# The last 256 feed-forward columns by seven products of quarters, and the products added up in a tree of bank copies

## The chip, the cores and the metric

The kernel runs on one core of a Trainium2 chip. The metric is the device time of one execution in microseconds (us). Before the change the median of three runs is 909.1 us (909.03 to 910.12).

Five engines take part, each with an instruction queue of its own that it works off in order: TensorE (PE, matmuls into PSUM banks), VectorE (DVE), ScalarE (ACT), GpSimd (POOL) and SyncE (SP). Here SP issues nearly all loads of weights; POOL issues those loads that add onto what a buffer holds.

## The reference

Two layers, each with a feed-forward stage, a mixing stage (attention, two kinds of heads) and a second feed-forward stage; 256 tokens of width 1024, feed-forward width 2816, all fp32. The change touches the four feed-forward stages alone:

```python
D_MODEL = 1024; SEQ = 256; DEPTH = 2; D_FF = 2816

def swiglu(h, w_gate, w_up, w_down):
    return (jax.nn.silu(h @ w_gate) * (h @ w_up)) @ w_down

for l in range(DEPTH):
    x = x + 0.5 * swiglu(rms_norm(x, ffn1_norm[l]), ffn1_w_gate[l], ffn1_w_up[l], ffn1_w_down[l])
    ...   # mixing stage: x = x + concat(oA, oB) @ W_out
    x = x + 0.5 * swiglu(rms_norm(x, ffn2_norm[l]), ffn2_w_gate[l], ffn2_w_up[l], ffn2_w_down[l])
return rms_norm(x, final_norm)
```

## The kernel before, in words

**Precision.** Every fp32 operand is held as two fp32r parts, high and low. A product of 128 rows is three matmuls: high by high, low by high, high by low. For a weight buffer (`raw`) ACT casts the high part and DVE subtracts it to get the low part; these are the tiles `w`, and one such half of a buffer (128x1024) is called a split. The 256 tokens stand in two blocks of 128.

**A feed-forward stage.** The 2816 columns go in five groups of 512 and a last 256. For each group the kernel makes gate and up products (over 1024 rows, in two halves of 512 rows), the hidden values silu(gate) x up, transposes them on PE, and adds the down product into four banks that stay open for the stage. The down product of a group comes one to two groups later: `below(old, g - 2, 1, ...)` is the right half (dn1) of the group two back, `below(by_token(new), g - 1, 0, ...)` the left half (dn0) of the group one back, for which the transposes (`turn_one`) are made and evicted in the same group: ACT copies the high part out of the bank, DVE takes the low part.

**Seven products of quarters.** Groups 1 to 4 (2 to 4 in the first stage) replace the eight products gate/up x two row halves x two token blocks by seven (`by_sevens`, Strassen's scheme in Winograd's form). The four quarters of the weights are a (gate, top rows), b (up, top), c (up, bottom), d (gate, bottom). The seven products take the weights a, d, c and the sums b+c, a+b, a+b+c, a+b+c+d; the x side has sums of its own (`q` and `v`), made in `make_sums`. Sums of weights are made in two ways: a *gather* is a load by POOL that adds b onto a's buffer once a has been split, or c onto b's once b has been loaded; the sums with c and with d are made by a DVE addition over the whole buffer (`raw<-raw,raw`, 128x2048).

**Order.** Each engine's instructions are recorded in program order; nothing reorders them afterwards. `specs` lists the weight buffers of the whole kernel as steps. `ahead(n)` splits buffers up to half-buffer n ahead of what PE has used, and with them issues the loads and the sums' preparation; how far ahead it runs at each place is read from the table `LEAD` by stage (`first`, `mid`, `last` for groups, `open`, `close`), through `go()`. So these numbers set where on DVE and ACT a split stands among the evictions. There are six `raw` buffers.

**The last 256 columns** go by plain products: one buffer holds 256 gate and 256 up columns side by side, so that one 512-wide matmul makes both. That is 24 matmuls for the top rows, the transposes of group 4 (`turn(h, 2)`, 8 of them), and 24 for the bottom rows:

```python
gu = pair()
tokens(gu, norm.xs, weights(), 0)
hT = turn(h, 2)
tokens(gu, norm.xs, weights(), 4)
h = hidden(gate([b[:, 0:256] for b in gu]), [b[:, 256:512] for b in gu])
```

Names in the profile: every engine instruction is recorded in one helper, line 62 before and line 77 after, so rows are told apart by tiles. `ps` and `xy` are PSUM banks, `w` weight parts, `raw` loaded weights, `s` tiles of x or of hidden values and their parts, `q` and `v` sums of x, `tmp` scratch for silu and sums, `hr` half of the norm factor.

## Time and profile before

| | before |
|---|---|
| median of three runs | 909.1 us |
| profiled execution: span | 907.5 us |
| its own time | 909.1 us: the span and some 1.6 us around it |
| PE busy | 899.1 us, 99% |
| DVE busy | 785.9 us, 87% |
| ACT busy | 609.8 us, 67% |
| POOL busy | 63.2 us, 7% |
| one group of 512 columns on PE, second stage | 30.8 us |
| last 256 columns on PE, second stage | 11.8 us |
| matmul and transpose instructions on PE | 4468 |

The page gives for each engine its busy time, the share of the span and the number of instructions. The chain that ended last is followed back from the last instruction, and an engine's share of it tells how much of the span hung on it. In a row of groups, "out<-in" names tiles, the numbers before the bar are shape and count, those behind it the busy us, the mean ns of one, and the idle time just before with the one who ended it. In a timeline, brackets at a row's end hold the idle time before it and who ended that. The granted PE clock is at full speed in all forty slices of the page.

The feed-forward stages lie at 8.7 to 188 us, 285.6 to 458.4, 458.4 to 634 and 731.4 to 896.5; the mixing stages are in between.

### The profile page before, as it was taken

The page shows a single profiled execution, that of the slowest core. Times are in us where ns is not written, and L with a number is a line of the kernel's source. Part 1 is how long each engine was busy: PE and PEld are TensorE (multiplying, and loading weights), DVE is VectorE, ACT ScalarE, POOL GpSimd, SP SyncE. Part 2 cuts the span into 40 slices and gives each one's busy share as a digit, 9 for nine tenths or more (in the row PEclk, how much of TensorE's full clock was granted, in tenths as well). Part 3 has the DMA queues.
Part 4 walks back from the last instruction along what each step waited for, and adds up shares of the span by engine and source line. Part 5 has one row for each costly group of instructions (what it writes and reads, how often), then busy time and mean ns, then how long its engine had stood idle before and what let it go on. Part 6 is the DMA issues. An engine that isn't in the chain of part 4 may idle for free.

```text
span 907.5 us, 12030 instructions
## 1 busy us (share of the span) xinstructions
PE 899.1 (99%) x4468; PEld 751.0 (83%) x4468; DVE 785.9 (87%) x1069; ACT 609.8 (67%) x970; POOL 63.2 (7%) x79
## 2 busy tenths in 40 slices
PE   9999999999999999999999999999999999999997
PEld 7888888888888888888888888888888888888886
DVE  5968999879987899999778999988888978999894
ACT  6946677666776776677575776667667785776660
POOL 0401000000001001000000001000000000101011
PEclk9999999999999999999999999999999999999999
DMA  9998897954148798897976898899611786898731
GB/s 328 355 287 213 236 309 247 268 143 179 47 150 241 174 265 247 247 300 256 279 204 171 250 278 258 252 303 248 182 57 48 263 223 166 234 312 255 219 114 47
DMA packets 114331, 200.83 MB, mean 221 GB/s; under 512 B 3678, under 2 KB 31648, under 8 KB 114272
## 3 DMA queue, kind: packets, MB, share of 16 engines
q1 hardware_dynamic: 97616, 167.66, 54.4%
q0 software_dynamic: 16096, 31.75, 20.1%
q8 instruction: 35, 0.57, 0.2%
q10 hardware_dynamic: 560, 0.66, 0.2%
q14 instruction: 24, 0.20, 0.1%
HBM read 199.00 MB, written 1.05 MB: 220 GB/s over the span
## 4 chain that ended last, share of the span: by engine, by line
PE 98%; DMA 1%; issue 0%; SPq 0%; DVE 0%; POOLq 0%; POOL 0%
PE ps L62 73%; PE xy L62 25%; DMA xk<-in_x_dram 1%; SPq L172 0%; DVE s L62 0%; DVE xk L62 0%; POOLq L1285 0%; POOL rf L62 0%; SPq L469 0%; SPq L465 0%; DVE tot L62 0%; DVE tmp L62 0%
## 5 line engine op out<-in xcount | busy, mean ns | idle before, releaser
L62 DVE TENSOR_TENSOR w<-raw,w 128x1024 fp32r<-128x1024 f32 (+1 forms) x458 | 476.4, 1097 | 34.6 <-ACT w L62 33.2
L62 PE MATMUL ps<-w,s 128*128 128x512 f32 (+1 forms) x2046 | 473.6, 389 | 0.0
L62 PEld LDWEIGHTS ps<-w,s 128*128 128x128 f32 x2046 | 379.9, 188 | 78.7 <-issue 0.8
L62 ACT CAST w<-raw 128x1024 fp32r<-128x1024 f32 (+1 forms) x457 | 403.9, 954 | 54.0 <-DVE raw L62 38.7
L62 PE MATMUL xy<-w,s 128*128 128x512 f32 x528 | 125.8, 392 | 0.0
L62 PEld LDWEIGHTS xy<-w,s 128*128 128x128 f32 x528 | 98.2, 188 | 20.4
L62 PE MATMUL xy<-w,q 128*128 128x512 f32 x360 | 88.1, 393 | 0.0
L62 PEld LDWEIGHTS xy<-w,q 128*128 128x128 f32 x360 | 66.5, 188 | 13.3
L62 PE MATMUL ps<-s,w 128*128 128x512 f32 (+1 forms) x384 | 69.8, 338 | 0.0
L62 DVE TENSOR_TENSOR raw<-raw,raw 128x2048 f32<-128x2048 f32 x30 | 68.6, 2288 | 0.5
L62 POOL DMA_DIRECT2D raw<-in_ffn_w_up_dram x30 | 38.9, 1313 | 430.1 <-DVE w L62 264.9
L62 PEld LDWEIGHTS ps<-s,w 128*128 128x128 f32 x384 | 58.6, 188 | 8.5
L62 ACT ACTIVATE s<-ps,gcol 128x256 fp32r<-128x256 f32 (+1 forms) x80 | 31.4, 479 | 34.0 <-PE ps L62 34.0
L62 ACT CAST s<-ps 128x512 fp32r<-128x512 f32 x36 | 20.4, 592 | 43.2 <-PE ps L62 43.0
L62 PE MATMUL ps<-w,q 128*128 128x512 f32 x180 | 43.2, 389 | 0.0
L62 PE MATMUL ps<-w,v 128*128 128x512 f32 x180 | 43.2, 389 | 0.0
L62 DVE TENSOR_TENSOR s<-ps,s 128x512 fp32r<-128x512 f32 x36 | 24.1, 686 | 19.5 <-ACT s L62 19.3
L62 PEld LDWEIGHTS ps<-w,v 128*128 128x128 f32 x180 | 33.8, 188 | 7.0
L62 PEld LDWEIGHTS ps<-w,q 128*128 128x128 f32 x180 | 33.8, 188 | 7.0
L62 ACT ACTIVATE s<-s,negm 128x256 f32<-128x256 f32 x64 | 31.8, 498 | 5.3 <-DVE negm L62 5.3
L62 ACT COPY ps<-ps 128x512 f32<-128x512 f32 x15 | 8.6, 570 | 34.4 <-PE ps L62 34.4
L62 DVE SCALAR_TENSOR_TENSOR s<-ps,gcol,s 128x256 fp32r<-128x256 f32 x48 | 20.3, 477 | 13.0 <-ACT s L62 12.9
(131 smaller groups left out, 584.3 us busy)
## 6 DMA issues: line engine op xcount, KB each, us to landing
raw<-in_ffn_w_down_dram SPq DMA_DIRECT2D x44, 1024.0 KB, 7.0
raw<-in_ffn_w_gate_dram SPq DMA_DIRECT2D x39, 1024.0 KB, 7.7
raw<-in_ffn_w_up_dram SPq DMA_DIRECT2D x39, 1024.0 KB, 7.1
raw<-in_ffn_w_up_dram POOLq DMA_DIRECT2D x30, 1024.0 KB, 10.0
raw<-in_w_in_dram SPq DMA_DIRECT2D x14, 1024.0 KB, 6.7
raw<-in_ffn_w_gate_dram SPq DMA_DIRECT2D x8, 512.0 KB, 7.9
raw<-in_ffn_w_up_dram SPq DMA_DIRECT2D x8, 512.0 KB, 8.9
raw<-in_w_in_dram SPq DMA_DIRECT2D x8, 512.0 KB, 6.0
```

What stands on the lines that cost most here:

```text
L62: ins = issue(*a, **k)
```

## The change

It has four parts.

1. **The last 256 columns go by seven products too.** Two buffers are loaded: r (the gate's 256 columns, top and bottom rows side by side) and q (up's). DVE makes all sums itself, on 128x4x256 halves. Seven products of 12 matmuls of 256 columns replace 48 of 512.
2. **Products accumulate in a tree of bank copies.** Four banks, A, B, Q and Y, are used over and over. The product with a is made in A, copied to Q and added to there by d: that is the first block's gate. a+b+c goes on into A, which is copied to Y, b+c into A again, which is copied to Q; c goes onto Y, a+b into B. The last product, a+b+c+d, goes onto Q and is the second block's gate at once, so one DVE subtraction per group falls away. The sign moves into `nhr`, minus half the norm factor.
3. **The weights of a group come in another order** (`ORDER`): a, dn1, d, dn0, a+b, a+b+c, b+c, c, a+b+c+d, before a, dn1, b+c, dn0, d, a+b, c, a+b+c, a+b+c+d. PE takes a+b+c ahead of a+b (`taker`). The gather c onto b is issued right behind the gather b onto a; before, some 10 us lay between them. c's own buffer is loaded beside the step of a+b (`also`).
4. **The table `LEAD` is new**, with entries for each stage and for the last 256 columns (`edge`); `make_sums` makes the sums of x in another order; the transposes of x go as matmuls with the transpose flag, one start and stop per bank.

The diff, cut; in `by_seven` the calls of `go()` and `flat()` are left out, and the words behind # are added here:

```diff
+ORDER = (("a", "d", "dn0", "ab", "abc", "bc", "c", "abcd"),
+         ("a", "dn1", "d", "dn0", "ab", "abc", "bc", "c", "abcd"))
...
-            mid=(2, 8, 12, 12, 15, 15, 20, 20, 20, 22, 23),
+            more1=(6, 9, 9, 11, 11, 15, 19, 19, 19, 24, 24),
+            edge1=(2, 7, 7, 9, 9, 11, 12, 12),
...
-        steps[0].prep = lambda: issue(gather(b, a), 1)
-        return [Step(4, 512, load(a), key=a, free=[])] + steps + [
-                Step(4, 512, None, src=a, free=[]),
-                Step(4, 512, load(c), key=c, free=[]),
-                Step(4, 512, None, prep=plus(c, a), src=a, free=[c], early=1),
-                Step(4, 512, None, prep=plus(d, a), src=a, free=[a, d])]
+        parts = dict(a=Step(4, 512, load(a), key=a, free=[]),
+                     d=Step(4, 512, load(d), key=d, free=[]),
+                     ab=Step(4, 512, None, src=a, free=[], also=(c, load(c))),
+                     abc=Step(4, 512, None, prep=plus(c, a), src=a, free=[]),
+                     bc=Step(4, 512, load(b), key=b, added=True),
+                     c=Step(4, 512, None, src=c, added=False),
+                     abcd=Step(4, 512, None, prep=plus(d, a), src=a, free=[a, d], early=2))
...
+        steps[steps.index(parts["a"]) + 1].prep = lambda: issue(gather(b, a), 1)
+        steps[steps.index(parts["d"]) + 1].prep = begin          # gather(c, b)
...
+    def small(wg, wu):
+        r, q = object(), object()
+        left, right = slice(0, 256), slice(256, 512)
+        def load(w):
+            return lambda t: [(t[:, :, h * 256:h * 256 + 256], rows(w, FF - 256, 256, 4 * h, 4)) for h in range(2)]
+        def plus(x, b, to, a):
+            dve.tensor_tensor(raws[to][:, :, a], raws[to][:, :, a], raws[x][:, :, b], op=ALU.add)
+        def pairs():
+            plus(q, left, r, left)
+            plus(q, right, q, left)
+        return [Step(4, 512, load(wg), key=r, src=r, free=[], pick=((r, left), (r, right))),
+                Step(4, 512, None, prep=pairs, src=r, free=[], also=(q, load(wu)), added=False, pick=((r, left), (q, left))),
+                Step(4, 512, None, prep=lambda: plus(q, right, r, left), src=r, free=[q], added=False, pick=((r, left), (q, right))),
+                Step(4, 512, None, prep=lambda: plus(r, right, r, left), src=r, free=[r], added=False, pick=((r, left), None))]
...
-                p1 = prod(norm.quarter(0, 0), take())
-                act.activation(xy[0], p1, AF.Copy, scale=-1.0)
...
-                g1 = flat()
-                dve.tensor_tensor(g1, p4, u1, op=ALU.subtract)
-                silu(g1, g1, 1)
+        def by_seven(banks, take, go, then):
+            A, B, Q, Y = banks
+            prod(norm.quarter(0, 0), take("a"), A, True)
+            act.copy(Q, A)
+            then("a")                                            # dn1, transposes
+            prod(norm.quarter(0, 1), take("d"), Q)
+            g0 = silu(flat(), Q, 0)
+            then("d")                                            # dn0
+            prod(norm.summed(1), take("abc"), A)
+            act.copy(Y, A)
+            prod(norm.summed(0), take("ab"), B, True)
+            act.copy(e, B)
+            prod(norm.summed(2), take("bc"), A)
+            act.copy(Q, A)
+            dve.tensor_tensor(u1, A, e, op=ALU.add)
+            prod(norm.summed(3), take("c"), Y)
+            dve.tensor_tensor(u0, Y, e, op=ALU.add)
+            up(h, u0, g0, 0, norm.nhr)
+            prod(norm.quarter(1, 1), take("abcd"), Q)
+            g1 = silu(flat(), Q, 1)
+            up(h, u1, g1, 1, norm.nhr)
...
-        gu = pair()
-        tokens(gu, norm.xs, weights(), 0)
-        hT = turn(h, 2)
-        tokens(gu, norm.xs, weights(), 4)
-        h = hidden(gate([b[:, 0:256] for b in gu]), [b[:, 256:512] for b in gu])
+            A, B, Q, Y = [b[:, 0:256] for b in banks]            # the same seven, 256 wide
+            wa = take()
+            prod(norm.quarter(0, 0), wa, 0, A, True)
+            act.copy(Q, A)
+            for t in range(2):
+                new.append(turn_one(h, t, banks[1 + 2 * t]))
+            prod(norm.quarter(0, 1), wa, 1, Q)
...
+            prod(norm.quarter(1, 1), take(), 0, Q)
```

**Three places in the instruction order.** First PE at the last 256 columns of the second feed-forward stage. Before, the end of the top rows' matmuls, the transposes of group 4 and the start of the bottom rows (`xy_4021` and `xy_4022` are the two token blocks' banks):

```order
L62 MATMUL xy_4022<-w_3965,s_525_2779 128x512 x2
L62 MATMUL xy_4022<-w_3966,s_525_2779 128x512
L62 MATMUL ps_4064<-ident,s_774_3949 128x128 x4
L62 MATMUL ps_4072<-ident,s_774_3949 128x128 x4
L62 MATMUL xy_4021<-w_3973,s_537_2834 128x512 x2
L62 MATMUL xy_4021<-w_3974,s_537_2834 128x512
L62 MATMUL xy_4022<-w_3973,s_537_2834 128x512 x2
L62 MATMUL xy_4022<-w_3974,s_537_2834 128x512
```

After, the end of the first product (a, in `ps_3039`), the transposes into the banks `xy_3041` and `xy_3042`, the product with d (into `ps_3040`) and the start of the third:

```order
L77 MATMUL ps_3039<-w_3932,s_523_2826 128x256 x2
L77 MATMUL ps_3039<-w_3933,s_523_2826 128x256
L77 MATMUL xy_3041<-ident,s_768_4000 128x128 x4
L77 MATMUL xy_3042<-ident,s_768_4000 128x128 x4
L77 MATMUL ps_3040<-w_3952,s_537_2885 128x256 x2
...
L77 MATMUL ps_3040<-w_3952,s_539_2895 128x256 x2
L77 MATMUL ps_3040<-w_3953,s_539_2895 128x256
L77 MATMUL ps_3039<-w_4016,q_2957 128x256 x2
L77 MATMUL ps_3039<-w_4017,q_2957 128x256
```

The matmuls are 256 wide, and the same four banks serve as in the groups.

Second DVE in group 4 of the same stage. Before, with `raw_3471` and `raw_3608` the down weights, `raw_3523` b with c on it, `raw_3659` d and `raw_3463` a, which at its end holds a+b:

```order
L62 TENSOR_TENSOR w_3710<-raw_3471,w_3709 128x1024
L62 TENSOR_TENSOR w_3714<-raw_3523,w_3713 128x1024
L62 SCALAR_TENSOR_TENSOR s_720_3693<-tmp_3689,hr_2897,tmp_3707 128x512
L62 TENSOR_TENSOR w_3722<-raw_3523,w_3721 128x1024
L62 TENSOR_TENSOR w_3767<-raw_3608,w_3766 128x1024
L62 TENSOR_TENSOR w_3771<-raw_3608,w_3770 128x1024
L62 TENSOR_TENSOR s_737_3782<-ps_3777,s_737_3782 128x512
L62 TENSOR_TENSOR s_738_3789<-xy_2999,s_738_3789 128x512
L62 TENSOR_TENSOR w_3793<-raw_3659,w_3792 128x1024
L62 TENSOR_TENSOR w_3797<-raw_3659,w_3796 128x1024
L62 TENSOR_TENSOR w_3801<-raw_3463,w_3800 128x1024
L62 TENSOR_TENSOR w_3805<-raw_3463,w_3804 128x1024
```

After, with `raw_3649` the weights of dn0, `raw_3501` a (from its third row here a+b, then with `raw_3681`, c, added), `raw_3683` b with c on it:

```order
L77 TENSOR_TENSOR w_3748<-raw_3649,w_3747 128x1024
L77 SCALAR_TENSOR_TENSOR s_709_3728<-tmp_3712,nhr_2950,tmp_3765 128x512
L77 TENSOR_TENSOR w_3806<-raw_3649,w_3805 128x1024
L77 TENSOR_TENSOR w_3810<-raw_3501,w_3809 128x1024
L77 TENSOR_TENSOR w_3814<-raw_3501,w_3813 128x1024
L77 TENSOR_TENSOR raw_3501<-raw_3501,raw_3681 128x2048
L77 TENSOR_TENSOR s_729_3825<-xy_3041,s_729_3825 128x512
L77 TENSOR_TENSOR s_730_3832<-xy_3042,s_730_3832 128x512
L77 TENSOR_TENSOR w_3836<-raw_3501,w_3835 128x1024
L77 TENSOR_TENSOR w_3840<-raw_3501,w_3839 128x1024
L77 TENSOR_TENSOR w_3844<-raw_3683,w_3843 128x1024
```

The two evictions of the transposes (`s<-ps,s` and `s<-xy,s` before, `s<-xy,s` after) stood ahead of the splits of a+b; now they stand behind these and behind the addition of c.

Third DVE at the last 256 columns. Before, splits of plain buffers and the evictions of the transposes:

```order
L62 TENSOR_TENSOR w_4002<-raw_3901,w_4001 128x1024
L62 TENSOR_TENSOR w_4024<-raw_3901,w_4023 128x1024
L62 TENSOR_TENSOR w_4028<-raw_3903,w_4027 128x1024
L62 TENSOR_TENSOR w_4032<-raw_3903,w_4031 128x1024
L62 TENSOR_TENSOR s_802_4069<-ps_4064,s_802_4069 128x2x256
L62 TENSOR_TENSOR s_804_4077<-ps_4072,s_804_4077 128x2x256
L62 SCALAR_TENSOR_TENSOR s_807_4108<-xy_4021,hr_2897,tmp_4104 128x256
L62 SCALAR_TENSOR_TENSOR s_807_4108<-xy_4022,hr_2897,tmp_4106 128x256
```

After, with `raw_3818` r and `raw_3856` q:

```order
L77 TENSOR_TENSOR w_3933<-raw_3818,w_3932 128x1024
L77 TENSOR_TENSOR w_3953<-raw_3818,w_3952 128x1024
L77 TENSOR_TENSOR raw_3818<-raw_3818,raw_3856 128x4x256
L77 TENSOR_TENSOR raw_3856<-raw_3856 128x4x256
L77 TENSOR_TENSOR tmp_3973<-ps_3039,tmp_3950 128x512
L77 TENSOR_TENSOR w_3976<-raw_3818,w_3975 128x1024
L77 TENSOR_TENSOR w_3980<-raw_3856,w_3979 128x1024
L77 TENSOR_TENSOR raw_3818<-raw_3818,raw_3856 128x4x256
L77 TENSOR_TENSOR tmp_3998<-xy_3042,tmp_3950 128x512
L77 SCALAR_TENSOR_TENSOR s_768_4000<-tmp_3998,nhr_2950,tmp_3871 128x512
L77 TENSOR_TENSOR w_4017<-raw_3818,w_4016 128x1024
```

Sums and splits of r and q alternate, with the two bank sums (`tmp`) and the hidden values (`s`) of group 4 among them.

More of the change, by code (lines that the diff above doesn't have):

```diff
@@ L129, in plain, with seven @@
         return Step(kn, n, lambda t: [(t, src)], **how)
-    def seven(wg, wu, c0, below, down):
+    def seven(wg, wu, c0, order):
         a, b, c, d = [object() for _ in range(4)]
@@ L296, in ffn_specs @@
                 if g in sevens:
[L297 removed]
+                    specs.extend(seven(wg[l], wu[l], g * 512, [dict(dn1=down(g - 2, 1) if g > 1 else None, dn0=downs[0]).get(o, o)
+                                                                  for o in ORDER[g > 1]]))
                     if g == max(sevens):
@@ L812, in turn @@
+        def turn(hs, n, into=None):
             out_ = []
-            for i in (range(n) if isinstance(n, int) else n):
-                sl = halves(bank())
+            for i in range(n):
+                sl = halves(into[i] if into else bank())
                 for c in range(2):
@@ L870, in ffn @@
             g = gate(gs)
-            next(sums)
         else:
```

308 lines of the change are left out of this document (185 added, 123 removed).

## Prediction

> **What bounds the kernel.** I read the page first (busy shares, then the shares of the chain that ended last), then what TensorE (PE) waited for.
>
> ```profile
> span 907.5 us, 12030 instructions
> PE 899.1 (99%) x4468; PEld 751.0 (83%) x4468; DVE 785.9 (87%) x1069; ACT 609.8 (67%) x970; POOL 63.2 (7%) x79
> PE 98%; DMA 1%; issue 0%; SPq 0%; DVE 0%; POOLq 0%; POOL 0%
> PE ps L62 <- DVE wake L62: 1.0, 1, 1.0
> PE ps L62 <- DMA xk<-in_x_dram: 0.7, 1, 0.7
> ```
>
> PE is on the chain for 98% of the span, and all its waits are two, 1.7 us together, in the opening. So nothing can be won by ending a wait: the change gains only what it takes off PE's stream, and loses whatever new wait it makes. VectorE (DVE) at 87% is the engine to watch, since the change gives it more to do and writes its work in another order.
>
> The chain in order of time shows PE's stream of the second feed-forward stage (start, length, what):
>
> ```profile
> 309.20 10.88 PE ps L62 x48
> ...
> 340.01 10.88 PE ps L62 x48
> ...
> 401.65 10.88 PE ps L62 x48
> ...
> 426.13 5.45 PE xy L62 x24
> 431.58 0.87 PE ps L62 x8
> 432.45 5.47 PE xy L62 x24
> 437.92 20.45 PE ps L62 x96
> ```
>
> From 309.20 one group of 512 columns takes 340.01 - 309.20 = 30.81 us. A 512-wide matmul costs 10.88 / 48 = 0.2267 us. From 426.13 to 437.92 the last 256 columns stand: 24 matmuls, 8 transposes of 0.87 us, 24 matmuls.
>
> **What PE saves.** Those 48 matmuls of 512 (10.88 us) become seven products of 12 matmuls each, 84 of 256. The transposes remain. The price of a 256-wide one is in a stretch of the mixing stage where four of each width alternate: one piece of the chain, and the forms in that window.
>
> ```profile
> 191.80 1.39 PE ps L62 x8
> L62 PE MATMUL ps<-s,w 128*128 128x512 f32 x4 | 1.4, 394 | 0.0
> L62 PE MATMUL ps<-s,w 128*128 128x256 f32 x4 | 1.1, 277 | 0.0
> ```
>
> (1.39 - 4 x 0.2267) / 4 = 0.121 us; by the difference of the two forms' own durations it is 0.2267 - (0.394 - 0.277) = 0.110 us. I take 0.12, since the first is a spacing and the second only a difference of modelled ends. 84 x 0.12 = 10.08 against 10.88: 0.80 us per stage, 3.2 us over four stages. The bounds are 4 x (10.88 - 84 x 0.121) = 2.9 and 4 x (10.88 - 84 x 0.110) = 6.6 us. Break-even is 10.88 / 84 = 0.1295 us a matmul.
>
> The page "TensorE: Matmul & The Clock Gate" of the Trainium skill, section "Back-to-back issue gap", gives a warm matmul as its columns over 2.4 GHz and about 2.5 ns. By that an estimate of the saving would be 1.2 us a stage, 4.7 us in all. This trace has 226.7 ns where that rule has 215.8, so the measured rows decide.
>
> In groups 1 to 4 (2 to 4 in the first stage) PE's count does not change: seven products and the same down products, only in another order.
>
> **What other engines get.** Their prices are in the groups by shape (count, busy us and mean ns, idle before and who ended it):
>
> ```profile
> L62 DVE TENSOR_TENSOR w<-raw,w 128x1024 fp32r<-128x1024 f32 x354 | 411.7, 1219 | 30.5 <-ACT w L62 29.3
> L62 DVE TENSOR_TENSOR raw<-raw,raw 128x2048 f32<-128x2048 f32 x30 | 68.6, 2288 | 0.5
> L62 DVE TENSOR_TENSOR tmp<-ps,tmp 128x512 f32<-128x512 f32 x15 | 10.3, 685 | 0.3
> L62 DVE TENSOR_TENSOR xk<-xk,ps 128x256 f32<-128x256 f32 x8 | 3.0, 416 | 1.9 <-PE ps L62 1.9
> L62 ACT CAST w<-raw 128x1024 fp32r<-128x1024 f32 x354 | 348.1, 1051 | 50.9 <-DVE raw L62 38.7 <-DMA raw<-in_ffn_w_up_dram 11.8
> L62 ACT COPY ps<-ps 128x512 f32<-128x512 f32 x15 | 8.6, 570 | 34.4 <-PE ps L62 34.4
> ```
>
> Each small stage gets three more weight splits (3 x 1.22 = 3.7 us of DVE, three casts of 1.05 on ScalarE), four half-width weight sums (half of 2.288: 1.14 each, 4.6 us), and two sums out of banks (0.84). Each group loses one subtraction of 0.685 (four in three stages, three in the first). So DVE gets 9.1 - 2.7 = 6.4 us more per stage, about 25 us in all, and 786 becomes some 811 of 906 us. Four `nhr` products a kernel are a few tenths. How full DVE is, stretch by stage:
>
> ```profile
> core 0: us, PE busy (x) PEld busy (x) DVE busy (x) ACT busy (x) POOL busy (x), PEclk, DMA share, GB/s
> 309.20:340.00 30.80, 30.80 (x142) 25.59 (x141) 28.92 (x27) 20.92 (x26) 1.28 (x1) 1.00 0.84 223
> 340.00:370.80 30.80, 30.80 (x142) 25.58 (x141) 29.50 (x28) 20.98 (x26) 2.57 (x2) 1.00 0.91 262
> 426.10:437.90 11.80, 11.80 (x58) 9.85 (x57) 9.69 (x10) 7.29 (x10) 0.00 (x0) 1.00 1.00 349
> 437.90:458.40 20.50, 20.50 (x98) 17.03 (x97) 17.24 (x21) 13.51 (x21) 1.31 (x1) 1.00 0.92 276
> ```
>
> The last two stretches have 32.3 us with 26.9 of DVE busy: 5.4 us free, and 9.1 come. The other 3.7 must be done ahead, in the groups before, which have one subtraction less each (2.7 together) and 1.3 to 1.9 us free each. It fits, with little left. I cost it at nothing; if the cover is gone, PE waits for splits of the closing down products, up to 3.7 us a stage.
>
> The tree of bank copies puts a ScalarE copy (0.57) between products that share a bank. Between them lies a full 512-wide product, 12 x 0.2267 = 2.7 us, or a 256-wide one of 12 x 0.12 = 1.44 us. The copy fits under both, unless it queues behind a cast of 1.05: 0.57 + 1.05 = 1.62 is 0.2 over 1.44. With four such places a stage I allow 0.2 us per stage at most, and none as the lower bound. SP's loads have the same bytes; c's and the up columns' loads are issued one step earlier beside another one.
>
> **The gather loop.** The larger risk is in DVE's order. A gather is a load by POOL that adds onto a buffer (b onto a, c onto b). Before, DVE evicts the two transposes for the next down product ahead of the splits of a+b; now (the order of group 4 shows it) those evictions stand behind both splits of a+b and the 2.2 us sum a+b+c. So the down product dn0, which stands early in the group, now hangs on the gather. Rows of before around one gather, DVE first, then POOL, ScalarE and the landing:
>
> ```profile
> 343.49 2.29 DVE L62 TENSOR_TENSOR raw<-raw,raw 128x2048 f32<-128x2048 f32 x1
> 345.69 3.57 DVE L62 TENSOR_TENSOR w<-raw,w 128x1024 fp32r<-128x1024 f32 x3
> ...
> 352.70 5.77 DVE L62 TENSOR_TENSOR w<-raw,w 128x1024 fp32r<-128x1024 f32 x5 [1.12 <-ACT w L62]
> ...
> 368.32 0.69 DVE L62 TENSOR_TENSOR s<-ps,s 128x512 fp32r<-128x512 f32 x1
> 368.92 0.68 DVE L62 TENSOR_TENSOR s<-xy,s 128x512 fp32r<-128x512 f32 x1
> 369.75 1.22 DVE L62 TENSOR_TENSOR w<-raw,w 128x1024 fp32r<-128x1024 f32 x1
> 371.72 1.23 DVE L62 TENSOR_TENSOR w<-raw,w 128x1024 fp32r<-128x1024 f32 x1 [0.74 <-ACT w L62]
> 326.66 1.28 POOL L62 DMA_DIRECT2D raw<-in_ffn_w_up_dram  x1 [19.90 <-DVE w L62]
> 357.63 1.28 POOL L62 DMA_DIRECT2D raw<-in_ffn_w_up_dram  x1 [8.88 <-DVE w L62]
> 370.63 2.00 ACT L62 CAST w<-raw 128x1024 fp32r<-128x1024 f32 x2 [0.91 <-DMA raw<-in_ffn_w_up_dram]
> L62 POOL DMA_DIRECT2D raw<-in_ffn_w_up_dram x1: 1283/1283/1283, 326.7 to 326.7; - x1
> DMA to landing us min/median/max: 8.4/8.4/8.4
> L62 POOL DMA_DIRECT2D raw<-in_ffn_w_up_dram x1: 1283/1283/1283, 357.6 to 357.6; - x1
> DMA to landing us min/median/max: 13.0/13.0/13.0
> ```
>
> The gather issued at 357.63 landed at 370.6, ScalarE had waited 0.91 us for it, DVE 0.74 us behind that. It cost PE nothing, because the evictions at 368.32 were already done. In the new order they would have come some 5.7 us later (one more cast, two splits and the sum). I call the time from issue to landing L.
>
> The loop from one a to the next a in DVE's queue: ten splits from a+b+c to the next a and two of a+b, 12 x 1.15 (5.77 / 5) = 13.8; two sums at 2.20 (345.69 - 343.49) = 4.4; the evictions 0.60 + 0.68 = 1.3; the wait from sum to cast to split 1.1; from a's split to the issue about 0.3; the cast of a+b 1.05; and L. That is 22.0 + L against PE's 30.8. It never stalls while L is 8.8 or less. Above that each of the two loops of a stage (groups 2 to 3 and 3 to 4) slips by L - 8.8; I let 1.7 us of slip be absorbed first, an estimate from walking group 1 with these spacings. A stage's stall is then 2 (L - 8.8) - 1.7: nothing at 9, 0.7 at 10, 2.7 at 11, 4.7 at 12.
>
> L is bounded by the rows: 8.4 for a gather whose neighbouring loads had little left, 13.0 for one in company. In the changed order the loads beside it are issued early (c beside a+b), and a second gather (c onto b) follows right behind on the same queue. I take 8.5 to 9.5, nearest to the row of 326.66, since the second of two gathers in a row should carry the delay, and it is not needed until b+c, some 17 us after.
>
> The page "DMA: Bandwidth & Descriptors" of the Trainium skill, section "Queues, rings and completion order", says that each DMA engine takes packets from its queues in turn, so a gather beside another load is stretched by what that one moves. The landings of 8.4 and 13.0 us agree with it. By that rule, with one load of 1 MB beside the gather, it is the first rival below.
>
> **Sum.** The profiled execution is 907.5 us of span and some 1.6 around it, which is the median of 909.1. 909.1 - 3.2 for the matmuls + 0.4 for copies and small waits (half of four stages' 0.2) = 906.3 us.
>
> **Rivals.**
> 1. The gather is late (slower). Speaking for it: the landing of 13.0, the queue pair now back to back, evictions behind a+b. Against: DVE has fewer things in the group, and the cover between a's splits and a+b is six splits, two bank sums and two products, 6 x 1.15 + 4 x 0.68 = 9.6 us, so a gather of up to 8.3 is not even seen. It decides from L = 10.1, where three stages' loss of 0.9 each takes all of the gain; from 10.4 (1.5 each) the kernel is slower by 0.2%. At L = 11: 906.3 + 3 x 2.7 = 914.4; at 12: 920.4. Halfway between the two landings, 10.7, which is how I read one load beside the gather, it is 906.3 + 3 x 2.1 = 912.6. I leave the first stage out: its group 1 goes without seven products, and by the same walk it enters the loop with some 4.6 us instead of 1.7.
> 2. No change that can be measured: the gain is eaten by copies behind casts and by closing splits that come late, 0.5 to 1 us per stage, 907.5 to 910. For it: 5.4 us free for 9.1; against: the lists of DVE work that can be done ahead.
> 3. 256-wide matmuls with their weight loads cost more in a row than among wide ones. At 0.14 us: 84 x 0.14 - 10.88 = 0.88 more per stage, 912.6. At the load's own busy time of 0.168 (751.0 / 4468), 84 x 0.168 = 14.1 and the time 922. Against it: the eight matmuls above have a load each and took 0.174 on average with half of them 512 wide.
>
> **Chances.** Forecast 906.3: 0.46 (904 to 907.3). Gather late: 0.27, 911 to 920. Gain eaten: 0.19. Dear 256-wide matmuls: 0.08. What a measurement of this kernel tells from no change is 0.2%, 1.8 us, so under 907.3 is faster and above 910.9 slower. Faster: the forecast, 0.45. Same: the eaten gain and the mild end of the late gather, 0.22. Slower: 0.33. The range, 904 to 917, takes in more than half of the way to the larger saving on PE (902.9) and a late gather up to L = 11.5.
>
> **What would show it.** Right: the seven products of the last 256 columns follow each other in about 10.1 us plus 0.87 of transposes, the group period stays 30.8, PE's waits stay under 3 us in all, the gathers of b onto a land within 9.5 us. Wrong by rival 1: PE waits for DVE's evictions (s) at the down products of groups 3 and 4, and landings above 10. By rival 2: waits for ScalarE's copies or DVE's splits (w) between the small products and in the closing. By rival 3: no waits, but the small products' pieces longer than 10.9 us.

## The result and the profile after

The changed kernel takes 935.1 us, median of 4 runs (932.67 to 936.18), against 909.2 us for the kernel before on the same chip: a ratio of 1.028 (95% interval 1.0266 to 1.0295). It is 26 us slower; 906.3 us was forecast. The profiled execution has a span of 934.3 us.

The page after: busy shares, and the shares of the chain that ended last.

```profile
PE 911.0 (98%) x4612; PEld 755.7 (81%) x4612; DVE 814.6 (87%) x1094; ACT 627.6 (67%) x998; POOL 60.6 (6%) x79
PE 55%; DMA 17%; DVE 15%; issue 6%; ACT 6%; POOL 0%; POOLq 0%; DVEq 0%; ACTq 0%
```

PE's span splits into busy and idle: before 899.1 busy and 8.4 idle, after 911.0 and 23.3. So 14.9 us of the loss are idle time and 11.9 us busy time: matmuls that take longer (the first set of experiments), and perhaps short waits that a modelled end hides. PE's share of the busy time fell by one per cent only; its share of the chain fell from 98% to 55%, and that is where the page shows a new bound: DMA, DVE and ACT in turn. PE's waits (us in total, times, longest):

```profile
PE ps L77 <- DVE s L77: 9.2, 10, 3.1
PE ps L77 <- ACT xy L77: 4.5, 5, 1.5
PE ps L77 <- ACT ps L77: 1.6, 3, 0.5
```

The first row is rival 1's sign: PE stands at a down product until DVE has evicted the transposes. The longest is in group 3 of the second stage; PE's waits of this row in groups 3 and 4 of the last three stages are 8.0 us. The chain (start, length, what) as it passes through the gather for group 4 of that stage:

```profile
398.25 10.18 DMA raw<-in_ffn_w_up_dram
408.45 1.06 ACT w L77
410.68 1.23 DVE w L77
411.93 2.29 DVE raw L77
414.22 0.61 DVE s L77
414.88 8.32 PE ps L77 x35
```

The timeline around the longest wait, by engine (POOL, ACT, DVE, PE), and the landing of the gather of 363.24:

```profile
363.24 1.28 POOL L77 DMA_DIRECT2D raw<-in_ffn_w_up_dram  x1 [27.52 <-DVE w L77]
398.25 1.28 POOL L77 DMA_DIRECT2D raw<-in_ffn_w_up_dram  x1 [28.09 <-DVE w L77]
...
375.18 2.00 ACT L77 CAST w<-raw 128x1024 fp32r<-128x1024 f32 x2 [4.39 <-DMA raw<-in_ffn_w_up_dram]
376.26 2.36 DVE L77 TENSOR_TENSOR w<-raw,w 128x1024 fp32r<-128x1024 f32 x2 [3.57 <-ACT w L77]
378.66 2.29 DVE L77 TENSOR_TENSOR raw<-raw,raw 128x2048 f32<-128x2048 f32 x1
380.87 1.28 DVE L77 TENSOR_TENSOR s<-xy,s 128x512 fp32r<-128x512 f32 x2
381.60 7.15 PE L77 MATMUL ps<-w,s 128*128 128x512 f32 x23 [3.15 <-DVE s L77]
DMA to landing us min/median/max: 11.9/11.9/11.9
```

And two windows: the time from that gather to the next, and the stretch after the wait (busy us of PE, PEld, DVE, ACT and POOL, with counts, then granted clock, DMA share and GB/s).

```profile
363.24:398.25 35.01, 31.86 (x136) 25.66 (x136) 29.11 (x27) 21.14 (x26) 2.57 (x3) 0.95 0.86 239
381.60:386.40 4.80, 4.80 (x14) 3.83 (x15) 3.86 (x4) 4.08 (x6) 0.00 (x0) 0.66 0.20 67
```

Read it as a loop. The gather b onto a is issued at 363.24 when DVE has split a. It lands 11.9 us later, at 375.16; ACT, idle for 4.39 us by then, casts; DVE, idle for 3.57 us, splits a+b, adds c, and only then evicts the transposes, while PE stands for 3.15 us. Everything behind in DVE's queue is late by then, the next group's a among it, and the next gather goes out at 398.25, 35.0 us after the last; PE's group takes about 31. The chain shows the same at that gather, which lands after 10.18 us. In the stretch after the wait PE's granted clock is 0.66: 14 matmuls in 4.80 us, where 21 fit at 0.2267.

What the last 256 columns cost, from the chain in order of time (products with d and a+b+c, then a+b, which reads `q`):

```profile
442.36 2.85 PE ps L77 x24
445.21 1.41 PE xy L77 x12
```

That is 0.1175 us a matmul at that product, where 0.12 was forecast. The two windows that hold the last 256 columns and the closing down products of this stage, as the prediction had them before (here they begin at 439.6, since the stage is late by then):

```profile
439.60:450.70 11.10, 11.05 (x93) 10.79 (x92) 10.58 (x13) 8.89 (x14) 0.00 (x0) 1.00 0.57 186
450.70:471.20 20.50, 20.50 (x99) 17.03 (x98) 20.35 (x26) 15.80 (x23) 0.00 (x0) 1.00 1.01 359
```

DVE is busy for 30.9 of 31.6 us there, and PE does not wait. The last 256 columns took 11.1 us of PE, 11.8 before.

### The profile page after: what moved, and what is told of

The parts are those of the page before. It is cut to its first block, busy times and chain, and to the rows that moved or that the text cites. A ratio compares the mean times of both kernels' runs of the same rounds, so it can differ in the third digit from the quotient of the medians.

```text
span 934.3 us, 12392 instructions
## 1 busy us (share of the span) xinstructions
PE 911.0 (98%) x4612; PEld 755.7 (81%) x4612; DVE 814.6 (87%) x1094; ACT 627.6 (67%) x998; POOL 60.6 (6%) x79
## 4 chain that ended last, share of the span: by engine, by line
PE 55%; DMA 17%; DVE 15%; issue 6%; ACT 6%; POOL 0%; POOLq 0%; DVEq 0%; ACTq 0%
PE ps L77 42%; DMA raw<-in_ffn_w_up_dram 17%; PE xy L77 14%; DVE w L77 8%; DVE raw L77 4%; ACT w L77 4%; DVE s L77 1%; DVE tmp L77 1%; ACT s L77 1%; ACT tmp L77 1%; ACT junk L77 0%; POOL raw L77 0%; ACT xy L77 0%; DVE ms L77 0%; DMA raw<-in_ffn_w_gate_dram 0%
## 5 line engine op out<-in xcount | busy, mean ns | idle before, releaser
L77 PE MATMUL ps<-w,s 128*128 128x512 f32 (+1 forms) x2094 | 480.5, 386 | 10.8 <-DVE s L77 9.2
L77 PE MATMUL ps<-w,q 128*128 128x512 f32 (+1 forms) x504 | 111.4, 372 | 4.5 <-ACT xy L77 4.5
L77 PEld LDWEIGHTS ps<-w,q 128*128 128x128 f32 x504 | 87.4, 188 | 23.8 <-ACT xy L77 6.4
L77 PE MATMUL xy<-w,s 128*128 128x512 f32 (+1 forms) x432 | 102.0, 387 | 0.0
L77 DVE TENSOR_TENSOR raw<-raw,raw 128x2048 f32<-128x2048 f32 (+1 forms) x38 | 78.4, 2063 | 0.5
L77 PE MATMUL xy<-w,v 128*128 128x512 f32 (+1 forms) x228 | 50.7, 371 | 0.0
L77 ACT ACTIVATE s<-ps,gcol 128x256 fp32r<-128x256 f32 (+1 forms) x80 | 31.4, 478 | 27.3 <-PE ps L77 26.1
L77 PEld LDWEIGHTS xy<-w,v 128*128 128x128 f32 x228 | 39.7, 188 | 8.2
L77 PE MATMUL xy<-w,q 128*128 128x512 f32 (+1 forms) x180 | 40.3, 373 | 0.0
L77 PEld LDWEIGHTS xy<-w,q 128*128 128x128 f32 x180 | 31.5, 188 | 6.5
L77 ACT ACTIVATE tmp<-ps,r 128x512 f32<-128x512 f32 (+1 forms) x40 | 25.6, 651 | 12.8 <-PE ps L77 10.5
L77 ACT CAST s<-xy 128x512 fp32r<-128x512 f32 x37 | 20.7, 587 | 15.1 <-PE xy L77 14.7
L77 ACT COPY xy<-ps 128x512 f32<-128x512 f32 (+1 forms) x27 | 14.3, 529 | 23.1 <-PE ps L77 22.2
```

What stands on the lines that cost most here:

```text
L77: ins = issue(*a, **k)
```

## The experiments

Sixteen kernels, timed against the kernel before with a 95% interval. Those of the third and fifth sets and e12_nosum leave out part of the computation, as their expectations say.

**First set: where the tiles lie.** Of the changed kernel's longer busy time one piece stands in the chain: twelve 512-wide matmuls with the sums `q` take 2.80 us, and 2.72 before, while those with `s` are unchanged. By the program's allocation `w`, `s`, `q` and `v` begin at 32 modulo 128 bytes in each partition before; the new tile `nhr` moves `q` and `v` alone by 64 bytes, to 96. One kernel undoes this in the changed kernel, one makes it in the kernel before, two move all tiles of the kernel before together.

```diff
 # e1_hr, from the changed kernel
-self.hr = tmp("hr", 2, (P, 2)); self.nhr = tmp("nhr", 2, (P, 2))
+both = tmp("hr", 2, (P, 4)); self.hr, self.nhr = both[:, 0:2], both[:, 2:4]
 # e2_pad, from the kernel before
+self.nhr = tmp("nhr", 2, (P, 2)); dve.tensor_scalar_mul(self.nhr, self.r, -0.5)
 # e13_pad32 (e14_pad96: P, 24), from the kernel before, ahead of all pools
+pad = const.tile([P, 8], F32, name="pad"); nc.vector.memset(pad, 0.0)
```

> The changed kernel with hr and nhr as the two halves of one tile, so that the sums of x (q and v) lie 64 bytes lower, where they lay before the change; nothing else differs. Theory 'place': 512-wide matmuls with q or v as their weights went from 0.2267 to 0.2333 us because these tiles moved by 64 bytes against the moving operand. Then the spacing is 0.2267 again and 720 x 0.0067 = 4.8 us go: about 930.3 us. Rival 'tree': the spacing comes from accumulating onto banks that ScalarE copies; then it stays at 0.233 and the time at 935.

> The kernel before, with the nhr tile added and written (8 bytes, unused), so that q and v move up by 64 bytes; nothing else differs. Theory 'place': its q and v products go from 0.2267 to 0.2333, 720 x 0.0067 = 4.8 us slower, about 913.9 us. Rival 'tree': no change, 909.1.

> The kernel before with 32 unused bytes ahead of the weight buffers, so that all of w, s, q and v lie 32 bytes higher (at 64 behind a multiple of 128 instead of 32). Theory 'relative': only the distance of the stationary tile to the moving one counts; spacing 0.2267 and time 909 as before. Rival 'absolute': a start at a multiple of 64 bytes is read faster; some 3000 matmuls of 512 columns at 0.216 instead of 0.2267 would make 30 us less, about 878.

> The same with 96 unused bytes, so that all these tiles start at a multiple of 128. Theory 'relative': 909. Rival 'absolute': as with 32 bytes or better, about 878; if only multiples of 128 count, this one alone is faster.

e1_hr took 930.7 us, 1.0241 (1.0225 to 1.0257); e2_pad 914.9, 1.0061 (1.0048 to 1.0074); e13_pad32 909.2 and e14_pad96 909.0, 0.9997 (0.9987 to 1.0007) and 0.9996 (0.9987 to 1.0006). The same product in the chain of the changed kernel, of e1_hr and of e2_pad:

```profile
423.20 2.80 PE xy L77 x12
```

```profile
421.44 2.72 PE xy L77 x12
```

```profile
321.55 2.80 PE xy L62 x12
```

So the move of `q` and `v` by 64 bytes is worth 4.4 us of the changed kernel's loss and 5.6 us in the kernel before; moving everything together by 32 or 96 bytes costs nothing. No run puts all tiles at 96, where `q` and `v` came to lie, so it is open whether their distance from the other tiles counts or their own place. The estimate is 15 groups x 48 matmuls x 0.0067 us = 4.8 us. Why these 64 bytes cost 6.7 ns a matmul no run here tells.

**Second set: mend DVE's and ACT's order.** e3_evict puts the evictions ahead of a+b again. e4_open puts the hidden values of group 0 ahead of a+b. e5_a_early, on top of e1_hr, splits the next group's a one place earlier, so that its gather goes out earlier. e6_both does as e5 and e4, with the sums of x earlier too.

```diff
 # e3_evict: LEAD
-more1=(6, 9, 9, 11, ...   last1=(2, 9, 9, 14, ...
+more1=(6, 7, 7, 11, ...   last1=(2, 7, 7, 14, ...
 # e4_open: LEAD
-next1=(11, 11, 14, ...    open1=(1, 0, 8, 6, 3, 11, 5, 1),
+next1=(8, 8, 14, ...      open1=(1, 0, 8, 6, 3, 9, 5, 1),
 # e5_a_early
+steps.insert(steps.index(parts["c"]), nxt[0])     # a of the next group
+nxt[1](parts["c"])                                # its gather
 # e6_both: e5_a_early with
+next1=(8, 8, 14, ...      open1=(1, 0, 8, 6, 3, 10, 5, 1),
+next(sums)                # twice, ahead of group 1
```

> The changed kernel with two numbers per group lowered from 9 to 7 in groups 2 to 4, so that VectorE's two evictions for dn0 stand ahead of the splits of a+b and of the sum a+b+c again; gathers and loads are issued as before. Theory 'loop': PE's waits at dn0 in groups 3 and 4 (9.7 us), in group 3 of the first stage, and the slow matmuls behind the two longest (3.9) go, about 13 us: 922 us; PE next waits, if at all, at a+b+c. Rival 'late gather': what PE lacks is a+b itself, so the waits move to the a+b+c or a+b products and the time stays above 930.

> The changed kernel with the numbers of the opening and of group 1 lowered in stages 1 to 3, so that VectorE's hidden values of group 0 stand ahead of the splits of a+b and the sum a+b+c. Theory 'order in group 1': of the 2.5 us that PE loses around group 1 in each of these stages, the 1.5 at the transposes, at the product with d and at dn0 go, the 0.85 to 1.0 at the copy into Y behind ScalarE's casts stay: 4.5 us in all, 930.5 us. Rival: the gather (landing at 303.0 in stage 1) is what is late; then the wait moves to a+b+c and the time stays at 934 or more.

> The changed kernel with hr and nhr in one tile (as in the run before), and with the a of each next group split one place earlier, ahead of c and a+b+c+d of the group before. Nothing else in the group's order is moved. Between a's split and the splits of a+b VectorE then has about 17 us of other work instead of 9.6. Theory 'loop': what slips in groups 3 and 4 is VectorE's queue, which stands still while it waits for the gather (23.1 us of its own and L of 9 to 12 against 31.1); with the cover the queue never stands, so PE's waits at dn0 in groups 3 and 4 and the slow matmuls behind them go (about 13 us): 930.7 - 13 = 918. Rival 'VectorE is simply full': its work per group plus its other waits is over 31 us, so the waits only move to other products and the time stays within 4 us of 930.7.

> As the run with a early, and in stages 1 to 3 also: the opening's and group 1's numbers lowered so that the hidden values of group 0 stand ahead of the sum a+b+c, and the sums of x made in five steps before group 1, as in the kernel before, instead of three before and two inside it. Theory: the wait of PE at ScalarE's copy into Y comes from the cast of v, which waits for VectorE's sums of x behind its splits; with these early the 2.5 us that PE loses around group 1 in each of three stages go: 918 - 7 = 911. Rival: group 1's wait is its gather, which is issued only when the norm factor is there; then the time is that of the run with a early, within 2 us.

All four are slower than the changed kernel: e3_evict 977.2 us (1.0747, 1.0727 to 1.0767), e4_open 954.1 (1.0496, 1.048 to 1.0512), e5_a_early 962.1 (1.0573, 1.0556 to 1.0591), e6_both 962.3 (1.0587, 1.0571 to 1.0602). In e3_evict DVE waits in its turn for the transposes that PE has not reached, and what stood behind is late (DVE, then ACT); PE's waits for ACT's copies into `xy` come to 25.7 us:

```profile
363.70 1.29 DVE L77 TENSOR_TENSOR s<-xy,s 128x512 fp32r<-128x512 f32 x2 [3.40 <-ACT s L77]
363.08 1.07 ACT L77 CAST s<-xy 128x512 fp32r<-128x512 f32 x2 [4.29 <-PE xy L77]
```

In e4_open the copy of bank A to Y stands on ACT behind the cast of `v`, which waits for DVE (PE, then ACT):

```profile
332.65 5.48 PE L77 MATMUL ps<-w,q 128*128 128x512 f32 x12 [6.49 <-ACT xy L77]
328.08 0.62 ACT L77 CAST v<-tmp 128x512 fp32r<-128x512 f32 x1 [4.84 <-DVE tmp L77]
332.02 0.58 ACT L77 COPY xy<-ps 128x512 f32<-128x512 f32 x1
```

In e5_a_early the wait for evictions is gone (0.6 us in all), and the other gather takes its place: the early a occupies a buffer, b is loaded late, c's gather onto it goes out late, and DVE stands for 4.62 us at b+c. PE then waits for copies (DVE, ACT, PE's waits):

```profile
361.13 6.90 DVE L77 TENSOR_TENSOR w<-raw,w 128x1024 fp32r<-128x1024 f32 x6 [4.62 <-ACT w L77]
360.05 3.91 ACT L77 CAST w<-raw 128x1024 fp32r<-128x1024 f32 x4 [4.40 <-DMA raw<-in_ffn_w_up_dram]
```

```profile
PE ps L77 <- ACT xy L77: 17.9, 6, 4.6
PE ps L77 <- ACT ps L77: 16.5, 12, 2.9
```

These runs say that the order written is a compromise, not that the wait for the gather is harmless. They can't price it: each makes a wait of its own.

**Third set: the gathers.** All from e1_hr, so that the place of `q` and `v` is out of the way. The gathers are left out, one kind or both, or the one from b onto a is halved.

```diff
-pool.dma_start(raws[to], w[k], accum_op=ALU.add)
+if not (k is b):          # e9_no_ab;  e9_no_bc: k is c;  e9_no_both: none
+    pool.dma_start(raws[to], w[k], accum_op=ALU.add)
 # e10_half
+n = 2 if k is b else 4
+pool.dma_start(raws[to][:, 0:n], w[k][:, 0:n], accum_op=ALU.add)
```

> The changed kernel with hr and nhr in one tile (930.7), leaving out the gathers b onto a (15 loads): a+b is then a, the rest is as it was. Theory 'two gathers in one queue': VectorE's queue loses the wait for a+b, but then stands for b+c (gather c onto b, which starts only when b is loaded), as in the run with a early; PE's waits at dn0 go, others come: 925 to 940. Rival 'a+b alone': all of PE's waits in groups 3 and 4 go, about 917.

> As the last, but leaving out the gathers c onto b instead (b+c is then b). The gathers b onto a then have the queue to themselves, and only the loads beside them. Theory 'two gathers in one queue': landings of 8.5 to 9.5 and no wait at b+c leave VectorE some 2 us less idle per group, and most of the waits in groups 3 and 4 go: about 920. Rival 'a+b alone': the waits at dn0 hang on a+b as before, and the time stays within 3 us of 930.7.

> As the last two, leaving out all 30 gathers. Every instruction of PE, VectorE and ScalarE is there, in the same order. Theory 'gathers': with no wait for a gather in VectorE's and ScalarE's queues PE's waits go, but for some at ScalarE's copies in group 1: 908 to 914, on the level of before. Rival 'VectorE is simply full, or the order by itself is bad': over 922.

> The changed kernel with hr and nhr in one tile (930.7 with whole gathers, 913.6 without those of b onto a); the gather b onto a brings only half of b (512 KB instead of 1 MB). Theory 'loop with a threshold': VectorE's queue needs 23.1 us and the landing L in each group of 30.8; with half the bytes L falls to some 6 to 8, the sum is under 31, and PE's waits at dn0 vanish as if there were no gather: 913 to 916. Rival 'bytes': the loss is the traffic's, half the bytes cost half of it, 922.

Without the gathers b onto a: 913.6 us, 1.0046 (1.0029 to 1.0062). Without c onto b: 923.9, 1.0178 (1.0116 to 1.0239). Without both: 913.5, 1.0048 (1.0033 to 1.0063). So the gathers b onto a cost 930.7 - 913.6 = 17.1 us; those from c onto b cost nothing of their own (913.5 against 913.6). Beside the gathers b onto a they may cost some 7 us (930.7 - 923.9), but that is not shown: the four runs without them lie between 920.5 and 933.7, and the interval overlaps that of e1_hr. PE, by the pages, is busy for 899.4 us and idle for 12.7 in e9_no_ab, in e1_hr 905.5 and 23.4: 11 us more idle and 6 more busy. By PE's waits in the two runs, of the 11 us 6.0 are waits for DVE's evictions and hidden values and 4.3 for ACT's copies. Of the 6 us about 2 are the lower clock after waits (mean granted 0.998 and 0.996 over 929 us, rounded); the other 4 are not assigned, and since the ends of matmuls are modelled, short waits can be in them. PE's waits in e9_no_ab, and the landings of the gathers b onto a in e9_no_bc:

```profile
PE ps L77 <- ACT xy L77: 4.6, 5, 1.2
PE ps L77 <- DVE s L77: 0.2, 1, 0.2
```

```profile
DMA to landing us min/median/max: 8.4/8.6/10.1
```

The wait for evictions is gone with the gather: it was the gather's. Alone on its queue the gather lands in 8.6 us (median), and the kernel still stands 10 us above e9_no_ab; in the profiled run, the fastest of its four, it is 6.4 us of span, with 2.1 us of waits for evictions.

e10_half took 920.1 us (914.86 to 921.62), 1.0108 (1.0078 to 1.0138): between the two expectations. In its profiled run (920.2 us) the landings in groups 2 to 4 of the third and fourth stage fell to 6.6 to 8.5 us, and PE's waits there are, but for 0.3 us, those of the kernel without gathers. What it loses against e9_no_both lies in the first two stages; in the first a new wait of 2.38 us at a copy stands, at 113.85. That fits a threshold above 8.5 us, but the total does not show it cleanly.

**Fourth set: the ending.** e7_plain_end is the changed kernel with plain products in the last 256 columns, with the old `close` numbers; e8_small is the kernel before with the seven small products alone; e12_nosum is e8_small without DVE's four weight sums in them.

```diff
 # e7_plain_end, in place of the seven small products
+tokens(gu, norm.xs, weights(), 0)
+hT = turn(h, 2, [A, Q])
+tokens(gu, norm.xs, weights(), 4)
 # e8_small, in the kernel before
-specs.append(Step(4, 512, gu_moves))
+specs.extend(small(wg[l], wu[l]))
 # e12_nosum, in small()'s plus
-dve.tensor_tensor(raws[to][:, :, a], raws[to][:, :, a], raws[x][:, :, b], op=ALU.add)
+pass
```

> The changed kernel with the last 256 columns by plain products again (48 matmuls of 512, one buffer of gate and up columns, the closing numbers of before); tree, weight order and the other numbers as changed. Theory: the seven products of 256 save 1.0 us of PE per stage (84 x 0.1175 against 10.88) and lose about 2.0 us in all by waits in that place, so without them the kernel is 1 to 3 us slower than the 935.1 of the changed one. Rival: the 9 us more of VectorE's work per stage is what makes PE wait; then it is faster, by the 5 us and more that VectorE lacks there, about 925.

> The kernel before with one part of the change alone: the last 256 columns by seven products of 256 with VectorE's sums (four banks, copies with the sign that the sums of x of before need). Groups, their order, gathers and numbers are those of before, the numbers at the end those of the changed kernel. Theory: this part saves 1.0 us of PE per stage and costs little where VectorE isn't late: 909.3 - 4.0 + 0 to 1.5 of waits, 905.3 to 906.8; so the loss of the whole change is the groups' new order. Rival: the 9 us more of VectorE's work per stage are not covered and PE waits in the closing, 909 to 913.

> The kernel before with the last 256 columns by seven products (939.9), leaving out VectorE's four sums of half-width weights in each stage (the products then take plain quarters). Theory 'VectorE late': what PE waits for there (4 to 5 us a stage at the copy behind ScalarE's casts, and the slow matmuls after it) comes from these sums in VectorE's queue, 4 x 1.14 us; without them it is gone or under 1 us a stage: 905.5 to 909. Rival 'order': the copy stands behind casts of loads anyway; then the time stays over 930.

e7_plain_end took 932.5 us, 1.0248 (1.0233 to 1.0263): 2.6 less than the changed kernel, with intervals that almost touch. So in the total the 3.2 us of the small products do not show. By the two traces the difference is not made at the ending: e7_plain_end is shorter by 4.4 and 1.9 us in the second and third stage and longer by 3.4 in the fourth. In the two shorter stages its gathers b onto a of groups 2 to 4 land in 8.5 to 8.7 us, and PE's groups keep to 31.2 to 31.4 us, though every gather is there at full size; in the changed kernel they take up to 36.3. In the fourth one lands in 11.5 us, and PE waits 3.39 us for the evictions behind it. PE's waits for evictions from group 2 of the second stage to the end of the third's groups (329 to 620 us), in the changed kernel and in e7_plain_end:

```profile
PE ps L77 <- DVE s L77: 5.4, 5, 3.1
```

```profile
PE ps L77 <- DVE s L77: 0.2, 1, 0.2
```

So in these stages it is the late landing that costs, and not the gather's bytes. What brings the landing forward there, the plain ending or chance, no run shows.

e8_small took 939.9 us, 1.0341 (1.0326 to 1.0357), e12_nosum 914.3, 1.0055 (1.004 to 1.007). In e8_small DVE, ACT and PE at the closing of the second stage:

```profile
441.24 1.22 DVE L64 TENSOR_TENSOR raw<-raw,raw 128x1024 f32<-128x1024 f32 x1
442.49 1.99 ACT L64 CAST w<-raw 128x1024 fp32r<-128x1024 f32 x2 [3.02 <-DVE raw L64]
444.38 0.36 ACT L64 COPY ps<-ps 128x256 f32<-128x256 f32 x1
444.80 2.93 PE L64 MATMUL ps<-w,s 128*128 128x256 f32 x12 [5.04 <-ACT ps L64]
```

The copy that PE waits for takes 0.36 us and was ready long before: it stands behind two casts, these wait for DVE's weight sum, and that is late. With the sums gone 25.6 us go. The order of e8_small was written for this experiment, so this says what a full DVE in the closing stretch can cost, not that it must. What e12_nosum keeps above the kernel before hangs in part on one wait for DVE, of 3.13 us, at 195.49 in the first mixing stage, with slow matmuls behind it.

**Fifth set: the copies.** What is left of PE's waits without gathers is mostly 0.8 to 0.9 us at a copy in group 1 of each of the last three stages, and 1.2 us at a copy in the last 256 columns of the first. ACT and then PE there, in the changed kernel:

```profile
322.11 0.62 ACT L77 CAST v<-tmp 128x512 fp32r<-128x512 f32 x1 [4.46 <-DVE tmp L77]
323.21 2.94 ACT L77 CAST w<-raw 128x1024 fp32r<-128x1024 f32 x3
326.06 0.58 ACT L77 COPY xy<-ps 128x512 f32<-128x512 f32 x1
326.69 3.06 PE L77 MATMUL ps<-w,q 128*128 128x512 f32 x12 [0.69 <-ACT xy L77]
```

The copy to Y stands behind the cast of `v`, which waits for a sum of x by DVE, and behind three weight casts. e11_sums, on e9_no_both, makes the sums of x in five steps, one more ahead of group 1:

```diff
 g = gate(gs)
+next(sums)
 h = hidden(g, us)
+if 1 in sevens: next(sums)
```

> The run without gathers (913.5), with the sums of x made in five steps before group 1, as in the kernel before, instead of partly inside it. Theory: PE's 1.0 us in group 1 of three stages, where it waits for ScalarE's copy into Y, comes from the cast of v ahead of it in ScalarE's queue; with the sums early it goes: 913.5 - 3 = 910.5. Rival: it is the casts of weights ahead of the copy; then no change, 913.5.

It took 921.9 us, 1.0131 (1.0114 to 1.0148). The same shape now stands at the other copy (ACT, then PE):

```profile
759.44 0.62 ACT L77 CAST v<-tmp 128x512 fp32r<-128x512 f32 x1 [1.30 <-DVE tmp L77]
759.96 1.98 ACT L77 CAST w<-raw 128x1024 fp32r<-128x1024 f32 x2
761.86 0.57 ACT L77 COPY ps<-ps 128x512 f32<-128x512 f32 x1
762.48 11.37 PE L77 MATMUL ps<-w,s 128*128 128x512 f32 x36 [2.97 <-ACT ps L77]
```

No kernel run here beats the kernel before.

## Why the prediction was wrong, point by point

**Where the 26 us are.** By differences of runs: place of `q` and `v` 935.1 - 930.7 = 4.4; gathers b onto a 930.7 - 913.6 = 17.1; what remains against the kernel before is 913.6 - 909.4 = 4.2. In that remainder the span grew by 4.6 us: PE's idle time went from 8.4 to 12.7 (4.3; the waits at ACT's copies are 5.0), and its busy time from 899.1 to 899.4, though some 3.2 us of matmuls had been taken off. A little slow clock (mean granted 0.998 against 0.999, 0.9 us) is in that; the other 2.6 us are not assigned.

**The saving on PE** was right in size: 0.120 us a 256-wide matmul in e9_no_ab, where `q` lies as before, and 0.1175 after, against 0.12. Rival 3, dear small matmuls, did not happen.

**"In groups 1 to 4 PE's count does not change"** is true, and the step taken from it, that their price does not either, is false: 0.2267 became 0.2333 us for the 720 matmuls with sums. The prediction had no term for it.

**The gather loop failed, as the largest term.** The 22.0 us besides L were about right; what failed are the landing L, the price of a late one, and the second gather, which stood at nothing.

The queue's own time, from ACT's cast at the landing to the next gather, is 855.86 - 833.62 = 22.2 us in the loop from 822.84 and 398.25 - 375.18 = 23.1 in the loop from 363.24. Most of the difference is a wait of DVE at the splits of b+c, behind a cast that waits for the other gather: c onto b, issued at 368.88, landed 15.4 us later.

```profile
833.62 2.00 ACT L77 CAST w<-raw 128x1024 fp32r<-128x1024 f32 x2 [2.25 <-DMA raw<-in_ffn_w_up_dram]
384.28 3.90 ACT L77 CAST w<-raw 128x1024 fp32r<-128x1024 f32 x4 [0.72 <-DMA raw<-in_ffn_w_up_dram]
385.37 4.63 DVE L77 TENSOR_TENSOR w<-raw,w 128x1024 fp32r<-128x1024 f32 x4 [0.94 <-ACT w L77]
```

The second gather was to be needed "some 17 us after" the first; in groups 2 to 4 of the last three stages it landed 16.3 to 21.0 us after the first was issued. With the first gather alone, and PE's group at 30.8 + 48 x 0.0067 = 31.1 at the dearer price, the loop should stall above L = 31.1 - 22.2 = 8.9. That this is the prediction's 8.8 is luck: the dearer matmuls made room for what the sum had left out.

The landing was taken as 8.5 to 9.5 us. In groups 2 to 4 of the last three stages the gathers b onto a took 9.1, 11.9 and 10.2, then 9.3, 9.9 and 9.6, then 8.8, 10.8 and 11.0. The trace of before could have warned: there, in the old order, the same nine took 8.4, 13.0 and 11.3, then 8.7, 10.7 and 12.5, then 8.5, 10.2 and 10.9, so six of nine lie above the 10.1 from which rival 1 was to decide. I read two of them. The page of before has the median of all thirty gathers, 10.0:

```profile
raw<-in_ffn_w_up_dram POOLq DMA_DIRECT2D x30, 1024.0 KB, 10.0
```

I chose the lower end because a second gather in a row should carry the delay. It carries one, and the first can be late all the same: without the second the first lands in 8.4 to 10.1 us (e9_no_bc), with it in 8.5 to 8.7 in two stages of e7_plain_end and in up to 11.9 in the changed kernel. The prediction's reading by the Trainium skill ("DMA: Bandwidth & Descriptors", "Queues, rings and completion order") was the nearer one, 10.7; but that section shares an engine's time among different queues, and the two gathers are on one, so it does not say how the second delays the first, nor does a run here. What makes one gather land in 8.7 us and the next in 11.9 is open.

Rival 1's price was too small as well. With the landings measured in groups 2 and 3 its formula gives 1.7, 0 and 0.3 us in the three stages; PE's waits for evictions in groups 3 and 4 are 8.0 us there, and the gathers b onto a cost 17.1 in all. The formula prices the first gather's slip alone: not the second gather's, not the waits at ACT's copies (4.3 of the 17.1), and not the lower clock after a wait (about 2). The first stage, which the rival left out, was not free either: from group 2 to group 3 PE took 33.8 us there, at a landing of 11.2. And 10 us remain in e9_no_bc, where most landings are near 8.6 and only 2.1 us of waits for evictions stand. What the rest of that is stays open.

**"The copy fits under both, unless it queues behind a cast"**: allowed 0.2 us a stage, found about 1. It queues behind three casts, and the first of the queue waits for DVE. I priced one ACT instruction by its length, where the queue in front of it had to be priced, with what the head of the queue waits for.

**"I cost it at nothing"**, DVE's 9.1 us in the closing against 5.4 free: right for the second stage, where DVE did 30.9 us in 31.6 and PE did not wait. That e7_plain_end was 2.6 us faster where it should have been 3.2 slower does not speak against it, since by the traces that lies in the groups, with the landings. e8_small shows a full DVE of this kind turning into 19 us of waits at ACT's copies.

**The chances** followed from L. With a threshold of 8.8 and L about 9, rival 1 was a matter of bad luck; with landings above 10 in six of nine gathers of the trace of before it had more than the 0.27 I gave it.

## What to carry to other kernels

Where a transfer is issued by what an engine's in-order queue has just done, and that same queue later waits for it, write down the loop: the queue's own work from issue to issue, every hand-over to another engine as often as it occurs, and the longest landing in the trace, read from every transfer of that kind and not from the one or two that seem nearest, and compare it with the period of the bounding engine; what that engine waits for behind it in the queue is late by the difference. A copy by another engine between two products ties the bounding engine to that engine's whole queue, so price the queue ahead of the copy. Before an order is mended by moving one entry, list who is waiting for the entries that get behind it: each of the five such moves here was slower than what it was to mend, with a new wait in another place.

## What the runs showed of the hardware

- An operand's place in the partition can change a matmul's price: with `q` and `v` moved by 64 bytes against the rest a 512-wide one took 0.2333 instead of 0.2267 us, and a 256-wide one 0.1175 instead of 0.120; moving all tiles by 32 or 96 bytes changed nothing.
- The granted clock fell after some short waits of PE. After the 3.15 us wait above it was 0.66 over 4.8 us; after one of 1.71 us in e1_hr, at 112.85, it stayed at 1.00 over the next 5 us. After one of 1.75 us, in the last stage of the changed kernel, it was 0.66 again:

```profile
873.29 7.14 PE L77 MATMUL ps<-w,s 128*128 128x512 f32 x23 [1.75 <-DVE s L77]
```

```profile
874.50:879.50 5.00, 5.00 (x16) 3.91 (x16) 4.71 (x5) 4.35 (x6) 0.00 (x0) 0.66 0.14 50
```

The page "TensorE: Matmul & The Clock Gate" of the Trainium skill, section "Part 1: The HAM clock gate (the "warmup" mystery)", lets the clock fall after an idle window of some 3.4 us. Here a wait of 1.75 us was once enough for a stretch of slow matmuls, and the trace decides.
